# Reordering queues around embedding tiles, the last MLP pair and the gate weights of a two-layer decoder trunk

## The chip, the cores and the metric

One core of one Trainium2 chip. The metric is the device time of one execution in microseconds; the time of a kernel is the median of its runs. TensorE (PE) multiplies, with a queue of weight loads (PEld) beside it; VectorE (DVE), ScalarE (ACT) and GpSimd (POOL) work on tiles; SyncE (SP) issues most DMA loads and stores.

## The reference, cut to what matters

Two layers on 512 tokens of 1024 features, everything in float32. Each layer has a mixer, an MLP and a gated embedding:

```python
for i in range(DEPTH):
    hn = rmsnorm(h, norm_mix_g[i])
    h = h + (even_mixer(hn, ...) if i % 2 == 0 else odd_mixer(hn, ...))
    hn = rmsnorm(h, norm_mlp_g[i])
    u = jnp.square(jax.nn.relu(hn @ w_mlp_up[i]))
    h = h + u @ w_mlp_down[i]
    gate = jax.nn.sigmoid(rmsnorm(h, norm_ple_g[i]) @ w_ple_gate[i])
    h = h + (p[i] @ w_ple_proj[i]) * gate
return rmsnorm(h, final_norm_g)
```

The even mixer has eight stick-breaking heads (groups 0 and 1 of four heads) and four differential heads (groups 2 and 3); the odd mixer has sixteen dilated attention heads.

## The kernel before

The residual stream `h` is kept transposed, as eight tiles of 128 features x 512 tokens. To keep float32 accuracy each factor of a matmul is split into a high part (a copy that rounds, on ACT) and a low part (the difference, on VectorE, or on GpSimd in the mixer), and each product is three matmuls, `mm3` (L138, L141, L142): high by high, low by high or high by low, and the other one. `wsplit` (L117 to L129) splits a block of weights that `wload` (L112) has brought in: the copy is L122, the difference L126 on GpSimd or L128 on VectorE. Raw weights have two buffers, split ones ("wh", "wl") three. `split_tile` (L175 to L184) does the same for a tile of `h`.

**Mixer.** `project` makes the values, queries and keys of one group while `attend` works on the group before; `interleave` mixes the two in program order. For each key tile `evacuate` (L478 to L499) scales the accumulator into one tile "tmp", and for each of its two heads makes two copies `kh` (L495, L496) on ACT and one difference `klz` (L497) on VectorE. In layer 0 `ple_units` (L355 to L373) follows directly behind the keys of groups 0 and 1: it multiplies the embedding by its projection, eight tiles of 128 x 512 one after another in the two "mm" banks; each is copied out by ACT (L372) and stored by SyncE (L373) for the gate stage.

**MLP.** The hidden features are worked in four chunks of four blocks. `up(ch, c)` makes two accumulators, each passed through a relu (L738, VectorE) and a square (L739, ACT), then differences T1 to T4 (L744 to L748, for a multiplication scheme with seven products in place of eight) and their split: `uh` (L750, ACT) and `ul` (L751, VectorE). `down(ch, c)` multiplies a chunk by its four w_down blocks; it sums and splits weights (L789 on ACT, L790 on VectorE), and the last one for a column block takes the last hidden block in a pass of its own, so that TensorE can begin before `uh` and `ul` are there. `side_sums` (L888) and `finished` add what was collected beside and split the finished tiles of `h` (L182, L183) for the next norm, whose squares are L241 and whose sums are L247 (a DMA add), L250, L251 and L254. `down_last` (L856 to L874) makes the last two tiles of `h` with plain products (L871).

**Gate.** Layer 0 (`ple_t`) takes the gate weights in four blocks and the accumulators as tiles of features; `Norm.finish` (L256 to L264) and `rsqrt` (L209 to L216: logarithm L210, exponential L213, then three VectorE steps L214, L215, L216) give the norm's root. Layer 1 (`ple_final`) turns to rows of tokens: for each half of the columns four split blocks, contracted in the order block, then token tile, in the first half, and token tile, then block, in the second; `turn` transposes `h` (L943, copied by L944), `tok_cols` (L281 to L287) transposes the root (L284) to a column per token tile, and the evacuation is sigmoid (L994), product (L995), sum (L996) and square (L997).

**What sets the order.** Each engine works through its queue in order. The queues are laid out ahead of time by the scheduler of the framework, which follows the program's order but lets a later instruction go first where, by its own reckoning, the earlier one isn't ready. `order(later, earlier)` (L224) pins two instructions of one engine against each other without a semaphore.

Of the kernel before, what the change touches and what calls it, by code (L numbers as in the profile page):

```python
# [62 lines left out]
def trunk(  # L63
# [53 lines left out]
    def wsplit(raw, i, nk, n, pool=None):  # L117
# [4 lines left out]
        nc.scalar.activation(hi, src, AF.Copy)  # L122
# [4 lines left out]
        else:  # L127
            nc.vector.tensor_tensor(lo, src, hi.bitcast(F32), op=ALU.subtract)  # L128
        return hi, lo  # L129

# [78 lines left out]
    def rsqrt(y, t, mean, eps, eps_t, scale=1.0, tables=None):  # L209
# [3 lines left out]
        nc.scalar.activation(y, y, AF.Exp, scale=-0.5)  # L213
        nc.vector.tensor_tensor(t, y, y, op=ALU.mult)  # L214
        nc.vector.scalar_tensor_tensor(t, mean, eps / scale, t, op0=ALU.add, op1=ALU.mult)  # L215
        nc.vector.scalar_tensor_tensor(y, t, 3.0 / scale, y, op0=ALU.subtract, op1=ALU.mult)  # L216
# [7 lines left out]
    def order(later, earlier):  # L224
        tc.add_manual_dep(
            later, earlier.name,
            mybir.DependencyInfo(mybir.DependencyClass.NoSync, mybir.DependencyReason.DATA),
            reason="activation tables")

    class Norm:  # L230
# [8 lines left out]
        def stats(self, k, after=(), dma=None, defer=None):  # L239
# [13 lines left out]
            else:  # L253
                nc.vector.tensor_tensor(self.acc, self.acc, sq, op=ALU.add)  # L254
# [100 lines left out]
    def ple_units(layer):  # L355
# [4 lines left out]
        for c in range(2):  # L360
            wh, wl = wsplit(raw, c, 2, 512)
            for i in range(4):
# [10 lines left out]
                nc.sync.dma_start(pjd[layer, 4 * c + i], t)  # L373

    KLB = 2
# [3 lines left out]
    def mixer(layer, norm, nxt):  # L379
# [35 lines left out]
        def project(g, cur):  # L415
# [62 lines left out]
            def evacuate(isq, i, acc, qk, qscale):  # L478
# [12 lines left out]
                else:  # L491
                    for s, (a, b) in enumerate(((lower, upper), (upper, lower))):
                        kl = klz[s][kl_i[0] % KLB]
                        kh = mpool.tile([P, S], F32R, tag="kh", name=nm("kh"), bufs=5)
                        nc.scalar.activation(kh[a], f[a], AF.Copy)  # L495
                        nc.scalar.activation(kh[b], f[a], AF.Copy)  # L496
                        nc.vector.tensor_tensor(kl[a], f[a], kh[a].bitcast(F32), op=ALU.subtract)  # L497
                        heads.append((qk[i][s], kh, kl))
                    kl_i[0] += 1  # L499
# [211 lines left out]
    def mlp(layer, fpool, norm, nxt):  # L711
# [4 lines left out]
        hidden, spare, stages, b12, low, lows = {}, [], [], [], [], []  # L716

        def up(ch, c):
# [16 lines left out]
            ul = fpool.tile([P, 7, HW], F32R, tag="ul", name=nm("ul"), bufs=5)  # L735
            for i, acc in enumerate(accs):
                ui = u[:, B11 + 2 * i:B11 + 2 * i + 2].rearrange("p a c -> p (a c)")
                nc.vector.scalar_tensor_tensor(ui, acc, 0.0, rstd[0], op0=ALU.max, op1=ALU.mult)  # L738
                nc.scalar.activation(ui, ui, AF.Square, scale=0.5)  # L739
# [8 lines left out]
            nc.vector.scalar_tensor_tensor(  # L748
# [3 lines left out]
            hidden[ch, c] = (uh, ul, part.ins)  # L752
# [9 lines left out]
        def down(ch, c):  # L762
# [19 lines left out]
            def split(src):  # L782
# [6 lines left out]
                nc.scalar.activation(hi, src, AF.Copy)  # L789
# [37 lines left out]
            w24 = split(s24)  # L827
            lows.append(low[0])
# [6 lines left out]
            for ks in ((0, 1, 2), (3,)) if last and c == 0 else (range(4),):  # L835
# [11 lines left out]
                if w is None:  # L847
                    w = split(rv[:, A12:A22 + 1])
                product(2, 0, w, 0, B21, False, True, ks)
# [6 lines left out]
        def down_last(c):  # L856
            blk = block(w_down[layer, 4 * (NCH - 1) + c], KT, P)
            low.clear()
            defer = []
            finished(c - 1)  # L860
            for i, (wh, wl) in enumerate(blk):
                acc = ps_wide()
                for m in range(4):
                    uh, ul = hidden[NCH - 1, m][:2]
                    bh, bl = b12[m]
                    for r, rows in enumerate((((acc[:, 0:HW], uh[:, B11], ul[:, B11]), (acc[:, HW:S], bh, bl)),
                                              ((acc, *(x[:, B21:B22 + 1].rearrange("p a c -> p (a c)") for x in (uh, ul))),))):
                        k = 2 * m + r
                        for lh, x in ((wh, 1), (wh, 2), (wl, 1)):
                            for row in rows:  # L870
                                nc.tensor.matmul(row[0], lh[:, k], row[x], start=k == 0 and x == 1 and lh is wh and row is rows[0],  # L871
                                                 stop=k == KT - 1 and lh is wl)
# [245 lines left out]
```

## Time and profile before

| | |
|---|---|
| median of 3 runs | 1305.18 us (1303.14 to 1307.39) |
| the profiled execution's own time | 1305.36 us |
| its span, first to last instruction | 1303.6 us |
| TensorE busy | 1277.1 us |
| VectorE, ACT, GpSimd busy | 1005.1, 710.2, 213.2 us |
| mean granted TensorE clock | 0.996 |

The span is the time from the first to the last instruction that the profiler saw. A timeline row gives the start, the duration, the engine, the line in the kernel, the operation, what it writes and reads, the shapes, and in brackets how long the engine had stood idle and whom it waited for. A row of the waits gives the total, the times and the longest.

### The profile page before, as it was taken

The numbers are of one execution on the slowest core, as the hardware profiler recorded it, in microseconds if no ns is written. First come the engines' busy times: TensorE is split into PE (matmuls) and PEld (weight loads), VectorE is DVE, ScalarE is ACT, GpSimd is POOL, SyncE is SP. The second block draws the span as 40 slices with busy tenths as digits, with TensorE's granted clock in tenths as the row PEclk, the third lists the DMA queues.
The fourth block names the chain that finished last, engine by engine and source line by source line (L and its number), as shares of the span: only waits on it lengthen the run. The fifth ranks groups of instructions, "written<-read, shape, count | busy, mean of one in ns | idle before, by whom it ended". The sixth has DMA issues, their size and how long they took to land.

```text
span 1303.6 us, 19326 instructions
## 1 busy us (share of the span) xinstructions
PE 1277.1 (98%) x7520; PEld 1125.7 (86%) x7520; DVE 1005.1 (77%) x1673; ACT 710.2 (54%) x1149; POOL 213.2 (16%) x184
## 2 busy tenths in 40 slices
PE   9999999999999999999999999999999999999996
PEld 7988887888988989988889888788899898998975
DVE  6788798778858869679767777887785885976876
ACT  6666867555535344355456666764553433534644
POOL 2433533400000000001023333231000000000201
PEclk9999999999999999999999999999999999999998
DMA  6421423222232322646432222212323133254741
GB/s 213 140 81 61 151 74 113 89 98 97 98 99 96 117 103 77 189 116 172 173 130 82 81 89 82 65 58 97 101 94 129 65 103 124 85 163 141 170 145 65
DMA packets 33996, 144.25 MB, mean 111 GB/s; under 512 B 3889, under 2 KB 4625, under 8 KB 21233
## 3 DMA queue, kind: packets, MB, share of 16 engines
q1 hardware_dynamic: 29680, 135.16, 30.6%
q0 software_dynamic: 4224, 7.87, 3.5%
q8 instruction: 59, 0.97, 0.3%
q14 instruction: 33, 0.26, 0.1%
HBM read 131.92 MB, written 6.37 MB: 106 GB/s over the span
## 4 chain that ended last, share of the span: by engine, by line
PE 76%; DVE 11%; ACT 5%; DMA 4%; issue 3%; POOL 0%; SPq 0%; ACTq 0%; DVEq 0%; POOLq 0%
PE mm L138 11%; PE mm L142 10%; PE mm L141 10%; PE sc L141 5%; PE sc L142 5%; PE sc L138 5%; PE pv L142 4%; PE pv L141 4%; PE pv L138 4%; PE tp L142 4%; PE tp L141 4%; PE tp L138 4%; PE pv L558 3%; PE tp L539 2%; DMA side<-u 2%
## 5 line engine op out<-in xcount | busy, mean ns | idle before, releaser
L122 ACT ACTIVATE wh<-raw 128x1024 fp32r<-128x1024 f32 (+1 forms) x156 | 160.5, 1034 | 142.7 <-PE mm L141 47.9
L126 POOL TENSOR_TENSOR wl<-raw,wh 128x512 fp32r<-128x512 f32 (+1 forms) x132 | 178.3, 1373 | 304.1 <-ACT wh L122 304.1
L138 PE MATMUL mm<-hi,wh 128*128 128x512 f32 x472 | 187.1, 396 | 0.2 <-ACT pjt L372 0.2
L142 PE MATMUL mm<-hi,wl 128*128 128x512 f32 x472 | 185.0, 392 | 1.6 <-DVE wl L128 1.5
L141 PE MATMUL mm<-lo,wh 128*128 128x512 f32 x472 | 184.6, 391 | 0.0
L128 DVE TENSOR_TENSOR wl<-raw,wh 128x1024 fp32r<-128x1024 f32 x90 | 109.4, 1221 | 46.4 <-ACT wh L122 40.8
L142 PEld LDWEIGHTS mm<-hi,wl 128*128 128x128 f32 x472 | 88.6, 188 | 22.2 <-DVE wl L128 2.2
L138 PEld LDWEIGHTS mm<-hi,wh 128*128 128x128 f32 x472 | 88.7, 188 | 16.8 <-ACT pjt L372 0.4
L141 PEld LDWEIGHTS mm<-lo,wh 128*128 128x128 f32 x472 | 88.8, 188 | 15.6
L760 POOL DMA_DIRECT2D s<-in_w_down_dram x4 | 4.5, 1123 | 579.1 <-DMA s<-in_w_down_dram 313.2
L789 ACT ACTIVATE wh<-s 128x1024 fp32r<-128x1024 f32 x58 | 61.1, 1053 | 52.8 <-DVE s L776 14.7
L751 DVE TENSOR_TENSOR ul<-u,uh 128x1792 fp32r<-128x1792 f32 x32 | 64.8, 2024 | 31.9 <-ACT uh L750 31.8
L533 ACT ACTIVATE e<-e,mn 128x128 f32<-128x128 f32 (+3 forms) x96 | 53.8, 561 | 62.3 <-DVE mn L530 61.9
L790 DVE TENSOR_TENSOR wl<-s,wh 128x1024 fp32r<-128x1024 f32 x58 | 70.8, 1221 | 13.9 <-ACT wh L789 13.5
L750 ACT ACTIVATE uh<-u 128x1792 fp32r<-128x1792 f32 x32 | 54.5, 1703 | 48.4 <-DVE u L748 48.2
L739 ACT ACTIVATE u<-u 128x512 f32<-128x512 f32 x64 | 39.7, 626 | 68.0 <-DVE u L738 67.8
L141 PE MATMUL sc<-lo,wh 128*128 128x512 f32 x184 | 72.1, 392 | 0.3 <-DVE lo L183 0.3
L138 PE MATMUL sc<-hi,wh 128*128 128x512 f32 x184 | 72.2, 392 | 0.1
L142 PE MATMUL sc<-hi,wl 128*128 128x512 f32 x184 | 71.9, 391 | 0.0
L138 PE MATMUL mm<-wh,hi 128*128 128x256 f32 (+1 forms) x216 | 63.2, 292 | 0.0
L142 PE MATMUL mm<-wh,lo 128*128 128x256 f32 (+1 forms) x216 | 62.9, 291 | 0.0
L141 PE MATMUL mm<-wl,hi 128*128 128x256 f32 (+1 forms) x216 | 62.8, 291 | 0.0
(305 smaller groups left out, 3887.1 us busy)
## 6 DMA issues: line engine op xcount, KB each, us to landing
raw<-in_w_up_dram SPq DMA_DIRECT2D x32, 1024.0 KB, 4.9
raw<-in_w_down_dram SPq DMA_DIRECT2D x32, 1024.0 KB, 4.9
raw<-in_w_in_dram SPq DMA_DIRECT2D x23, 1024.0 KB, 4.9
raw<-in_w_gate_dram SPq DMA_DIRECT2D x8, 1024.0 KB, 6.0
bias<-urow SPq DMA_DIRECT2D x24, 256.0 KB, 3.6
raw<-in_w_outa_dram SPq DMA_DIRECT2D x8, 768.0 KB, 4.2
pj<-pjd SPq DMA_DIRECT2D x16, 256.0 KB, 5.7
h<-in_xT_dram SPq DMA_DIRECT2D x8, 256.0 KB, 5.7
```

Of the source, the lines that this page charges most:

```text
L122: nc.scalar.activation(hi, src, AF.Copy)
L126: nc.gpsimd.tensor_tensor(lo[:, kx], src[:, kx], hi[:, kx].bitcast(F32), op=ALU.subtract)
L128: nc.vector.tensor_tensor(lo, src, hi.bitcast(F32), op=ALU.subtract)
L138: mm = nc.tensor.matmul(acc, lh, rh, start=start, stop=False)
L141: nc.tensor.matmul(acc, lh, rl, start=False, stop=False)
L142: return mm.ins, nc.tensor.matmul(acc, ll, rh, start=False, stop=stop).ins
L533: nc.scalar.activation(e[:, 0:n], e[:, 0:n], AF.Exp, scale=-1.0, bias=mn, accum_out=s)
L739: nc.scalar.activation(ui, ui, AF.Square, scale=0.5)
L750: nc.scalar.activation(uh, u, AF.Copy)
L751: part = nc.vector.tensor_tensor(ul, u, uh.bitcast(F32), op=ALU.subtract)
L789: nc.scalar.activation(hi, src, AF.Copy)
L790: low[:] = [nc.vector.tensor_tensor(lo, src, hi.bitcast(F32), op=ALU.subtract).ins]
```

## The change

It has three parts. First, in layer 0 the copies of the last key tile's second head of groups 0 and 1 (and the difference behind them) are no longer emitted with the first head's, but by `ple_units` just behind the first embedding tile's copy and store. Second, in the MLP the low half of the second weight pair of `down(3, 0)` is ordered behind the first relu of `up(3, 3)`, the high half of its third pair behind the second square and the low half of that behind T4. Third, `down_last` loads and splits the first gate block itself, between its two accumulators; `finished(2)` comes behind that, its side sums ordered behind the first gate low half, the squares' sums behind the second. In layer 1 the last gate block's splits are ordered behind the root (high halves behind the exponential, low halves behind the last step), two of the split blocks swap pools, and `tok_cols` is emitted behind two token tiles of the fourth block instead of ahead of it.

```diff
@@ ple_units, mixer @@
                 nc.sync.dma_start(pjd[layer, 4 * c + i], t)
+                while late_copies:
+                    late_copies.pop()()
...
-                        nc.scalar.activation(kh[a], f[a], AF.Copy)
-                        nc.scalar.activation(kh[b], f[a], AF.Copy)
-                        nc.vector.tensor_tensor(kl[a], f[a], kh[a].bitcast(F32), op=ALU.subtract)
+
+                        def copies(a=a, b=b, kh=kh, kl=kl):
+                            nc.scalar.activation(kh[a], f[a], AF.Copy)
+                            nc.scalar.activation(kh[b], f[a], AF.Copy)
+                            nc.vector.tensor_tensor(kl[a], f[a], kh[a].bitcast(F32), op=ALU.subtract)
+
                         heads.append((qk[i][s], kh, kl))
+                        if i and s and layer == 0 and g in groups[2:]:
+                            late_copies.append(copies)
+                        else:
+                            copies()
@@ Norm.stats @@
-                nc.vector.tensor_tensor(self.acc, self.acc, sq, op=ALU.add)
+                add = nc.vector.tensor_tensor(self.acc, self.acc, sq, op=ALU.add)
+                for a in late_add:
+                    order(add.ins, a)
@@ up, down @@
-                nc.vector.scalar_tensor_tensor(ui, acc, 0.0, rstd[0], op0=ALU.max, op1=ALU.mult)
-                nc.scalar.activation(ui, ui, AF.Square, scale=0.5)
+                chain.append(nc.vector.scalar_tensor_tensor(ui, acc, 0.0, rstd[0], op0=ALU.max, op1=ALU.mult).ins)
+                chain.append(nc.scalar.activation(ui, ui, AF.Square, scale=0.5).ins)
...
-            hidden[ch, c] = (uh, ul, part.ins)
+            hidden[ch, c] = (uh, ul, part.ins, chain[0], chain[3], t4.ins)
...
             w24 = split(s24)
+            if last and c == 0:
+                order(low[0], hidden[ch, 3][3])
...
                     w = split(rv[:, A12:A22 + 1])
+                    if last and c == 0:
+                        order(high[0], hidden[ch, 3][4])
+                        order(low[0], hidden[ch, 3][5])
@@ down_last @@
-            low.clear()
             defer = []
-            finished(c - 1)
...
+                if i == 0:
+                    raw = wload(w_gate[layer, 0])
+                    n = (KT, P) if layer < DEPTH - 1 else (2, 512)
+                    gate.append(wsplit(raw, 0, *n))
+                    low[:] = last_low
+                    gate.append(wsplit(raw, 1, *n))
+                    late_add[:] = last_low
+                    finished(c - 1)
                 nc.vector.tensor_tensor(h[2 * c + i], h[2 * c + i], acc, op=ALU.add)
                 nxt.done(2 * c + i, defer=defer)
+            late_add.clear()
@@ ple_t @@
-            blk = block(w_gate[layer, c], KT, P)
+            blk = gate if c == 0 else block(w_gate[layer, c], KT, P)
@@ ple_final @@
-            gw = []
-            for half in range(2):
+            gw = [] if c else list(gate)
+            for half in range(1 - c, 2):
                 raw = wload(w_gate[layer, 2 * c + half])
                 for b in range(2):
-                    gw.append(wsplit(raw, b, 2, 512, pool=fpool if c else None))
+                    gw.append(wsplit(raw, b, 2, 512, pool=None if (c, half, b) in ((0, 1, 0), (1, 1, 1)) else fpool))
+                    if c and half:
+                        order(last_high[0], root[0])
+                        order(last_low[0], root[1])
...
                     for t in range(QT):
                         contract(t, b, 0)
+                        if b == 3 and t == 1:
+                            rcol = tok_cols(rstd)
...
                     if b == 2:
-                        rcol = tok_cols(norm.finish())
+                        rstd = norm.finish()
                         turn(1)
```

`last_low`, `last_high` and `root` hold the instructions of the latest `wsplit` and `rsqrt`.

21 lines of the change are left out of this document (14 added, 7 removed).

## The prediction

> **What bounds the kernel now.** I read the page first, then the waits of TensorE, then the timeline of each engine around each wait that the edits touch.
>
> ```profile
> PE 1277.1 (98%) x7520; PEld 1125.7 (86%) x7520; DVE 1005.1 (77%) x1673; ACT 710.2 (54%) x1149; POOL 213.2 (16%) x184
> ```
>
> TensorE is busy for 98% of the span, so the change, which removes no arithmetic, can only return time in which TensorE stands still. The waits of TensorE say how much that is and who ends it (total us, times, longest):
>
> ```profile
> PE mm L138 <- ACT tmp L372: 2.6, 2, 1.4
> PE mm L141 <- DVE ul L751: 2.0, 2, 1.0
> PE tp L284 <- DVE rstd L216: 1.7, 1, 1.7
> ...
> PE mm L142 <- DVE wl L128: 1.5, 1, 1.5
> ...
> PE mm L142 <- DVE wl L790: 0.8, 2, 0.4
> ```
>
> Each of the first four belongs to one part of the diff, so I take them as parts A, B, E and D. The fifth (C, in the third w_down pair) isn't edited, but comes just behind B.
>
> **A: the last key tile's second head.** The two waits are at the start of the two embedding runs, in layer 0. The first:
>
> ```profile
> 140.59 0.63 ACT L495 ACTIVATE kh<-tmp 64x512 fp32r<-64x512 f32 x1
> 141.24 0.63 ACT L496 ACTIVATE kh<-tmp 64x512 fp32r<-64x512 f32 x1
> 141.78 0.57 ACT L372 ACTIVATE tmp<-mm 128x512 f32<-128x512 f32 x1
> ...
> 141.00 0.22 PE L516 MATMUL sc<-masks 128*128 128x128 f32 x1
> 142.40 0.50 PE L138 MATMUL mm<-wh,wh 128*128 128x512 f32 x1 [1.18 <-ACT tmp L372]
> 142.74 0.39 PE L141 MATMUL mm<-wl,wh 128*128 128x512 f32 x1
> 142.97 0.40 PE L142 MATMUL mm<-wh,wl 128*128 128x512 f32 x1
> ```
>
> The third embedding tile needs one of two "mm" banks; the copy that frees it (L372) stands on ACT behind the two copies of the second head (140.59 and 141.24). With those two deferred, L372 starts at 140.59 and ends at 141.16. The second site has the same order:
>
> ```profile
> 203.28 0.63 ACT L495 ACTIVATE kh<-tmp 64x512 fp32r<-64x512 f32 x1
> ...
> 204.46 0.57 ACT L372 ACTIVATE tmp<-mm 128x512 f32<-128x512 f32 x1
> ...
> 203.36 0.33 PE L513 MATMUL sc<-kh,qq 128*128 128x256 f32 x1
> 205.09 0.50 PE L138 MATMUL mm<-wh,wh 128*128 128x512 f32 x1 [1.40 <-ACT tmp L372]
> ```
>
> There L372 would end at 203.28 + 0.57 = 203.85 instead of 205.03.
>
> What a wait costs is more than its bracket. Rows of L138 to L142 with 512 columns last 0.39 and start 0.23 apart (142.74 to 142.97), so 0.16 of a matmul normally lies under the next one; and the first one behind the wait is followed after 0.34 (142.40 to 142.74), 0.11 more than normal. So each wait costs its bracket plus 0.27, by starts alone. The Trainium skill ("Perfetto Trace Analysis", section on the Tensor Engine Instruction) says that the end of a matmul row is estimated from its size and not observed; the trace agrees, as the rows overlap. By the brackets alone A, B, D and E would sum to 7.75, by starts to 9.26.
>
> A by starts: 1.18 + 1.40 + 2 × 0.27 = 3.12. What is late next: TensorE is free at about 141.05 and 203.55, so 0.1 and 0.3 of a wait stay. And the deferred pair (2 × 0.65 by its spacing) now stands ahead of the second embedding tile's copy: 141.16 + 1.30 + 0.57 = 143.0, where the fourth tile asks for its bank at 141.2 + 6 × 0.23 = 142.6. That is up to 0.4 per site. I take 0.55 returned per site, A = 2.0; ends 0.8 and 3.1. The deferred VectorE subtraction goes with the copies; the scores of that head are twelve steps away, and SyncE's store of the first embedding tile only moves earlier.
>
> **B: orders around the last pair.** Layer 1, last up block and the first w_down block behind it:
>
> ```profile
> 1195.39 1.22 DVE L790 TENSOR_TENSOR wl<-s,wh 128x1024 fp32r<-128x1024 f32 x1
> 1196.53 0.69 DVE L738 SCALAR_TENSOR_TENSOR u<-pv,rstd 128x512 f32<-128x512 f32 x1
> ...
> 1199.37 1.23 DVE L790 TENSOR_TENSOR wl<-raw,wh 128x1024 fp32r<-128x1024 f32 x1
> 1200.51 0.69 DVE L744 TENSOR_TENSOR u<-u 128x512 f32<-128x512 f32 x1
> ...
> 1202.21 1.70 ACT L750 ACTIVATE uh<-u 128x1792 fp32r<-128x1792 f32 x1 [2.10 <-DVE u L748]
> ...
> 1203.94 2.02 DVE L751 TENSOR_TENSOR ul<-u,uh 128x1792 fp32r<-128x1792 f32 x1 [1.83 <-ACT uh L750]
> ...
> 1197.15 0.28 PE L138 MATMUL mm<-uh,wh 128*128 128x256 f32 x1
> ...
> 1204.70 0.28 PE L138 MATMUL mm<-uh,wh 128*128 128x256 f32 x1
> 1206.03 0.39 PE L141 MATMUL mm<-ul,wh 128*128 128x256 f32 x1 [1.04 <-DVE ul L751]
> ```
>
> The chain to ul is relu (L738), square, differences, L750, L751. Two low halves of weights (1195.39 and 1199.37, 1.2 each) stand in it. The orders put the first behind the first relu, the second behind the last difference, where VectorE waits 1.83 for L750 anyway. The first relu starts at 1195.39; the second one's accumulator is complete just behind 1197.15, where the w_down block begins, so with some 0.5 for what VectorE still does there it ends near 1198.4. Its square is as long as the relu (0.7), the differences take 1202.21 - 1200.51 = 1.70 up to L750: near 1200.8. L750 1.70 and L751 2.02 end near 1204.6, before 1204.98 where ul is wanted. Who waits for the moved halves: the first now ends near 1196.53 + 0.69 + 0.1 = 1197.3, and its product comes third in the w_down block, behind two of nine matmuls each; the 63 matmuls from 1197.15 to 1204.70 start 0.12 apart, so at 1199.3. The second ends near 1200.8 + 1.23 = 1202.0; its product is the sixth, at 1197.15 + 45 × 0.12 = 1202.6. The raw buffer that it releases comes free 1.4 later, and with it the next SyncE load, whose block begins only after all of this one. Behind the halves on VectorE and ACT stand only members of the same chain. B by starts: 1.97 + 2 × 0.27 = 2.51; I take 2.4, ends 0 (the chain moves by nothing) and 2.5.
>
> C starts from TensorE's own results (copies out of the banks, a DMA add, side sums), so it should move along. If it is bound by loads instead, it grows by what B saves. I charge 0.5 for both layers; ends +1.3 (0.8 + 2 × 0.27 gone) and -2.4 (all of B given back).
>
> **D: early gate weights.**
>
> ```profile
> 610.04 1.04 ACT L122 ACTIVATE wh<-raw 128x1024 fp32r<-128x1024 f32 x1
> ...
> 614.58 1.22 DVE L128 TENSOR_TENSOR wl<-raw,wh 128x1024 fp32r<-128x1024 f32 x1
> ...
> 607.43 0.28 PE L871 MATMUL tp<-uh,wh 128*128 128x256 f32 x1
> ...
> 613.07 0.39 PE L138 MATMUL mm<-hi,wh 128*128 128x512 f32 x1
> ...
> 615.85 0.50 PE L142 MATMUL mm<-hi,wl 128*128 128x512 f32 x1 [1.46 <-DVE wl L128]
> ```
>
> In layer 0 the second gate block's low half is made at 614.58, though its high half ended at 611.08: h updates and splits are ahead of it on VectorE. Emitted in the middle of the last w_down block and with the squares' adds ordered behind it, it needs only its load, which keeps its place, and the weight buffer that the first half of that block frees at 607.43, where the second begins. So it ends near 607.6 + 1.04 + 1.22 = 609.9, ahead of the gate product at 613.07, and 1.46 + 0.27 = 1.73 goes. What is now behind the first gate low half, the side sums of tiles 4 and 5 and with them their splits, is wanted by the fifth of eight steps of the gate product, 4 × 6 × 0.23 = 5.5 behind 613.07; behind the second stand only sums for the norm, which is read after the whole product. Tiles 4 and 5 use no DMA add, so POOL isn't concerned. In layer 1 there is no such wait and I count 0. D = 1.7, ends 1.0 and 1.8.
>
> **E: the last gate block behind the root.**
>
> ```profile
> 1259.80 2.01 ACT L122 ACTIVATE wh<-raw 128x1024 fp32r<-128x1024 f32 x2 [8.68 <-DMA raw<-in_w_gate_dram]
> 1261.71 0.67 ACT L210 ACTIVATE rstd<-tp,eps_n 128x512 f32<-128x512 f32 x1
> ...
> 1264.61 0.69 DVE L216 SCALAR_TENSOR_TENSOR rstd<-e,rstd 128x512 f32<-128x512 f32 x1
> ...
> 1259.64 0.40 PE L262 MATMUL tp<-e,ones_r 128*128 128x512 f32 x1
> ...
> 1265.45 0.63 PE L284 MATMUL tp<-ident,rstd 128*128 128x128 f32 x4 [1.74 <-DVE rstd L216]
> ```
>
> ```profile
> L944 DVE COPY ht<-tp 128x512 f32<-128x512 f32 x8 | 5.3, 687 | 0.6 <-PE tp L943 0.6
> ```
>
> The two high halves run ahead of the logarithm, whose input is complete at 1259.64 + 0.40 and a little, say 1260.1. Ordered behind the root they give 1261.71 - 1260.1 = 1.6: rstd is ready near 1263.7 instead of 1265.3, and moving tok_cols behind two token tiles of the fourth contraction lets transposes of h go first. E by starts: 1.74 + 0.16 = 1.90 (no refill there, as the transposes are short); I take 1.4, because h copies of 0.69 (L944) may now slip between the root's three steps; ends 0.5 and 1.9. The new places of two split blocks (one out of the shared weight buffers, one into them) I count at nothing: the block that leaves them no longer waits for a buffer, so the load behind it, which landed at 1259.8, comes earlier, and its split is now held by the root in any case.
>
> **Sum.** 2.0 + 2.4 - 0.5 + 1.7 + 1.4 = 7.0. The profiled execution took 1305.36, 0.18 above the median 1305.18 of the runs; its waits stand for all. So 1298.4 for such an execution, 1298.2 as the median, 0.54% less. A measurement of this kernel can tell about 0.3% (3.9 us) from no change.
>
> **The rivals.** One: waits change hands. The deferred pair blocks the fourth embedding tile, and the pair's low halves or C give B back. For it: ACT's rows at both sites of A follow each other without a gap, and C lies one block behind B. Against: the room reckoned above. D and E stay: 1305.18 - 3.1 = 1302.1.
>
> Two, slower: the low halves of the last gate block, now behind the root, fall behind the evacuation of the first 512 columns, whose adds come earlier in the program.
>
> ```profile
> 1269.63 0.40 PE L138 MATMUL tp<-wh,hi 128*128 128x512 f32 x1
> ...
> 1279.53 0.69 DVE L996 TENSOR_TENSOR ht<-ht,gt 128x512 f32<-128x512 f32 x1
> ```
>
> The last column tiles begin at 1269.63 and want the halves after twelve matmuls, at 1272.4. Made behind the last add they are ready at 1280.2 + 2 × 1.22 = 1282.6: a wait of 10.2, so 1298.2 + 10.2 = 1308.4, with A and C at their poor ends up to 1311.5. It decides once the halves end after 1272.4, that is, from the second evacuated token tile on. Against it: the halves can be made as soon as the root is there, before rcol exists and so before any sigmoid. The Trainium skill ("TensorE: Matmul & The Clock Gate", architectural detail) says that ScalarE and VectorE take their queues strictly in order; the trace agrees at 141.78, and by that rule nothing can overtake a half that is placed late.
>
> Three: the deferral and the orders leave the queues as they are, and only D acts: 1305.18 - 1.7 = 1303.5.
>
> **How the numbers follow.** Forecast 0.72 (0.70 of it over 0.3% faster), rival one 0.16 (0.02 faster, 0.14 within), rival two 0.07 (0.05 slower, 0.02 within), rival three 0.05 (within). Faster 0.72, same 0.23, slower 0.05. The low end is all 9.26 returned and nothing given back, 1295.9. The high end takes in rival one with its 0.5 of spread, 1302.6; rivals two and three are outside.
>
> **What would show it.** In the waits of TensorE, L372, L751, L216 and L128 gone or under 0.5 each; L372 ahead of the second head's L495; L738 ahead of the first L790; L128 for the second gate block ending before 611; L210 ahead of the last two L122. A new wait on L372 or a larger one on L790 would mean rival one; a wait of TensorE on L128 behind 1265 would mean rival two. A TensorE busy time that differs from 1277.1 by more than 2 would make the whole reckoning wrong.

## The result, and the profile after

| | before | after |
|---|---|---|
| median | 1305.07 us (6 runs, 1303.14 to 1307.39) | 1296.33 us (6 runs, 1295.27 to 1298.25) |
| ratio to before | | 0.9932, 95% interval 0.992 to 0.9945 |
| the profiled execution, its span | 1305.36, 1303.6 | 1296.47, 1294.7 |
| end of the last matmul, stretch from there to the end of the span | 1291.87, 11.68 | 1285.31, 9.39 |

The change is faster by 8.7 us, 0.68%. The forecast was 1298.2 in a range of 1295.9 to 1302.6. The sum of 7.0 fell short by 1.7, and not because every term was a little small. Between the two profiled executions the last matmul ends 6.56 us earlier, 0.44 less than the sum. The other 2.29 us lie behind the last matmul, in a place that the prediction did not look at.

The page of the changed kernel first, then its waits of TensorE (total us, times, longest):

```profile
PE 1277.1 (99%) x7520; PEld 1125.5 (87%) x7520; DVE 1003.3 (77%) x1673; ACT 710.0 (55%) x1149; POOL 212.5 (16%) x184
```

```profile
PE mm L141 <- ACT tmp L381: 1.1, 2, 0.8
...
PE mm L145 <- DVE wl L810: 0.7, 2, 0.4
...
PE mm L144 <- DVE ul L771: 0.2, 1, 0.2
```

(The lines have moved: the three matmuls of `mm3`, L138, L141 and L142, are now L141, L144 and L145, L247 is now L254, L372 is L381, L495 and L496 are L509 and L510, L738 is L758, L790 is L810, L750 and L751 are L770 and L771, L210 to L216 are L213 to L219, L284 is L293, L943 and L944 are L976 and L977, L950 is L983, L994 to L997 are L1032 to L1035, L254 is L261, the "fin" steps of L272 are L281.) TensorE is as busy as before, so the reckoning in idle time holds. The wait on the root (L216) and the one on the gate's low half (L128) are gone, L751's 2.0 is 0.2, C's 0.8 is 0.7. Of A's 2.6 there is still 1.1. Take the same matmul in both traces by its number in TensorE's order: the lead is how much earlier it starts after the change. It grows to 1.25 by 280 us (A), from 1.27 to 2.08 at 578 (B, layer 0), from 1.99 to 3.74 at 616 (D), from 3.57 to 4.42 at 1206 (B, layer 1), from 4.54 to 4.86 at 1253 (a wait on a copy of h that is gone), and from there to 6.56 at the last matmul (E). Between these places it drifts by 0.1 to 0.2.

The timeline of the changed kernel at the four places:

```profile
140.52 0.60 ACT L381 ACTIVATE tmp<-mm 128x512 f32<-128x512 f32 x1
...
141.14 0.63 ACT L509 ACTIVATE kh<-tmp 64x512 fp32r<-64x512 f32 x1
...
141.17 0.50 PE L141 MATMUL mm<-wh,wh 128*128 128x512 f32 x1 [0.37 <-ACT tmp L381]
...
142.96 0.19 PEld L141 LDWEIGHTS mm<-wh,wh 128*128 128x128 f32 x1 [0.33 <-ACT pjt L381]
142.96 0.50 PE L141 MATMUL mm<-wh,wh 128*128 128x512 f32 x1
...
202.24 0.61 ACT L510 ACTIVATE kh<-tmp 64x512 fp32r<-64x512 f32 x1
...
202.88 0.60 ACT L381 ACTIVATE tmp<-mm 128x512 f32<-128x512 f32 x1
...
203.53 0.50 PE L141 MATMUL mm<-wh,wh 128*128 128x512 f32 x1 [0.77 <-ACT tmp L381]
...
608.43 1.22 DVE L128 TENSOR_TENSOR wl<-raw,wh 128x1024 fp32r<-128x1024 f32 x1
...
1192.46 0.69 DVE L758 SCALAR_TENSOR_TENSOR u<-pv,rstd 128x512 f32<-128x512 f32 x1
1193.07 1.21 DVE L810 TENSOR_TENSOR wl<-s,wh 128x1024 fp32r<-128x1024 f32 x1
...
1197.62 1.22 DVE L810 TENSOR_TENSOR wl<-raw,wh 128x1024 fp32r<-128x1024 f32 x1
1197.79 1.70 ACT L770 ACTIVATE uh<-u 128x1792 fp32r<-128x1792 f32 x1 [0.78 <-DVE u L768]
...
1201.61 0.39 PE L144 MATMUL mm<-ul,wh 128*128 128x256 f32 x1 [0.20 <-DVE ul L771]
...
1255.20 0.69 ACT L213 ACTIVATE rstd<-tp,eps_n 128x512 f32<-128x512 f32 x1 [10.16 <-PE tp L271]
...
1256.46 1.99 ACT L122 ACTIVATE wh<-raw 128x1024 fp32r<-128x1024 f32 x2
1256.59 0.69 DVE L217 TENSOR_TENSOR e<-rstd 128x512 f32<-128x512 f32 x1 [0.26 <-ACT rstd L216]
1257.20 0.68 DVE L977 COPY ht<-tp 128x512 f32<-128x512 f32 x1
...
1259.24 0.68 DVE L219 SCALAR_TENSOR_TENSOR rstd<-e,rstd 128x512 f32<-128x512 f32 x1
...
1260.07 0.63 PE L293 MATMUL tp<-ident,rstd 128*128 128x128 f32 x4
```

Each order that the prediction asked to see is there: the embedding copy ahead of the second head's copies, the first relu ahead of the low half, the gate's low half done before 611, the logarithm ahead of the last two high halves. One of its signs isn't met: of the waits that were to go or fall under 0.5, the second one on L381 is 0.77. Three places are to be kept in mind: at the first site of A the fourth embedding tile (142.96) has waited for its bank (the 0.33 of its weight load), at the second site the first head's second copy (202.24) stands ahead of L381, and a copy of h (1257.20) has slipped between the root's steps.

Where the unforeseen 2.29 come from is seen in the last evacuation. Before, ScalarE and the last matmul:

```profile
1283.57 0.73 ACT L950 ACTIVATE ht<-ht,fin 128x512 f32<-128x512 f32 x1 [2.60 <-DVE fin L272]
1284.20 0.67 ACT L994 ACTIVATE gt<-tp,rcol 128x512 f32<-128x512 f32 x1
...
1289.68 0.72 ACT L950 ACTIVATE ht<-ht,fin 128x512 f32<-128x512 f32 x1 [2.60 <-DVE fin L272]
1290.31 0.67 ACT L994 ACTIVATE gt<-pv,rcol 128x512 f32<-128x512 f32 x1
...
1291.60 0.28 PE L142 MATMUL mm<-wh,lo 128*128 128x256 f32 x1
...
1295.02 0.45 ACT L994 ACTIVATE gt<-mm,rcol 128x256 f32<-128x256 f32 x1
```

After:

```profile
1274.68 0.67 ACT L1032 ACTIVATE gt<-tp,rcol 128x512 f32<-128x512 f32 x1
...
1278.39 0.73 ACT L983 ACTIVATE ht<-ht,fin 128x512 f32<-128x512 f32 x1 [0.18 <-DVE fin L281]
...
1279.66 0.69 ACT L1032 ACTIVATE gt<-pv,rcol 128x512 f32<-128x512 f32 x1 [0.54 <-PE pv L145]
...
1285.04 0.28 PE L145 MATMUL mm<-wh,lo 128*128 128x256 f32 x1
...
1286.16 0.46 ACT L1032 ACTIVATE gt<-mm,rcol 128x256 f32<-128x256 f32 x1
```

Before, each scaled copy (L950) waits 2.60 for a chain of small VectorE steps ("fin") and the next tile's sigmoid stands behind it; the sigmoids come 1290.31 - 1284.20 = 6.1 apart. The last one starts 3.4 behind the start of the last matmul. The Trainium skill ("TensorE: Matmul & The Clock Gate", architectural detail) says that ScalarE takes its queue strictly in order; the trace agrees, since a sigmoid starts right behind each scaled copy (1284.20 behind 1283.57, 1290.31 behind 1289.68). After, the second tile's sigmoid (1274.68) stands ahead of the first tile's scaled copy (1278.39), the third's waits for TensorE itself (0.54 on pv), and the last one starts 1.1 behind the start of the last matmul. No line of the diff names these instructions.

### The profile page after: what moved, and what is told of

Its sections match the earlier page's. It is cut to its first block, busy times and chain, and to the rows that moved or that the text cites. A ratio compares the mean times of both kernels' runs of the same rounds, so it can differ in the third digit from the quotient of the medians.

```text
span 1294.7 us, 19322 instructions
## 1 busy us (share of the span) xinstructions
PE 1277.1 (99%) x7520; PEld 1125.5 (87%) x7520; DVE 1003.3 (77%) x1673; ACT 710.0 (55%) x1149; POOL 212.5 (16%) x184
## 4 chain that ended last, share of the span: by engine, by line
PE 80%; DVE 10%; ACT 4%; DMA 2%; issue 2%; POOL 0%; SPq 0%; ACTq 0%; DVEq 0%; POOLq 0%
PE mm L141 11%; PE mm L144 11%; PE mm L145 11%; PE sc L144 5%; PE sc L145 5%; PE sc L141 5%; PE pv L145 4%; PE pv L144 4%; PE pv L141 4%; PE tp L145 4%; PE tp L144 4%; PE tp L141 4%; PE pv L577 3%; PE tp L558 2%; PE tp L894 2%
## 5 line engine op out<-in xcount | busy, mean ns | idle before, releaser
L141 PE MATMUL mm<-hi,wh 128*128 128x512 f32 x472 | 187.1, 396 | 0.2 <-ACT pjt L381 0.2
L145 PE MATMUL mm<-hi,wl 128*128 128x512 f32 x472 | 184.8, 391 | 0.1
L144 PE MATMUL mm<-lo,wh 128*128 128x512 f32 x472 | 184.6, 391 | 0.0
L128 DVE TENSOR_TENSOR wl<-raw,wh 128x1024 fp32r<-128x1024 f32 x90 | 109.6, 1222 | 39.6 <-ACT wh L122 34.1
L145 PEld LDWEIGHTS mm<-hi,wl 128*128 128x128 f32 x472 | 88.6, 188 | 20.0 <-POOL wl L126 0.5
L141 PEld LDWEIGHTS mm<-hi,wh 128*128 128x128 f32 x472 | 88.7, 188 | 16.9 <-ACT pjt L381 0.4
L144 PEld LDWEIGHTS mm<-lo,wh 128*128 128x128 f32 x472 | 88.8, 188 | 15.5
L771 DVE TENSOR_TENSOR ul<-u,uh 128x1792 fp32r<-128x1792 f32 x32 | 64.8, 2024 | 29.6 <-ACT uh L770 29.5
L810 DVE TENSOR_TENSOR wl<-s,wh 128x1024 fp32r<-128x1024 f32 x58 | 70.8, 1221 | 12.6 <-ACT wh L809 12.2
L770 ACT ACTIVATE uh<-u 128x1792 fp32r<-128x1792 f32 x32 | 54.5, 1703 | 45.7 <-DVE u L768 45.4
L144 PE MATMUL sc<-lo,wh 128*128 128x512 f32 x184 | 72.3, 393 | 0.4 <-DVE lo L186 0.4
L141 PE MATMUL sc<-hi,wh 128*128 128x512 f32 x184 | 72.2, 392 | 0.0
L145 PE MATMUL sc<-hi,wl 128*128 128x512 f32 x184 | 71.9, 391 | 0.0
L141 PE MATMUL mm<-wh,hi 128*128 128x256 f32 (+1 forms) x216 | 63.4, 293 | 0.0
L145 PE MATMUL mm<-wh,lo 128*128 128x256 f32 (+1 forms) x216 | 63.0, 292 | 0.0
L144 PE MATMUL mm<-wl,hi 128*128 128x256 f32 (+1 forms) x216 | 62.9, 291 | 0.0
```

The lines of the kernel that those rows point to most:

```text
L128: last_low[:] = [nc.vector.tensor_tensor(lo, src, hi.bitcast(F32), op=ALU.subtract).ins]
L141: mm = nc.tensor.matmul(acc, lh, rh, start=start, stop=False)
L144: nc.tensor.matmul(acc, lh, rl, start=False, stop=False)
L145: return mm.ins, nc.tensor.matmul(acc, ll, rh, start=False, stop=stop).ins
L770: nc.scalar.activation(uh, u, AF.Copy)
L771: part = nc.vector.tensor_tensor(ul, u, uh.bitcast(F32), op=ALU.subtract)
```

## The experiments

Two questions were open: what each part is worth by itself, and what shortened the stretch behind the last matmul. Theory T said ScalarE's queue order there; the rival R said the earlier root and evacuation. Times of a set stand beside runs of the kernel before in the same set: 1306.89 (17 runs) for the first four, 1306.79 (11) for the next four, 1306.53 (13) for the last four. The changed kernel, run again in the last set, is the yardstick for times (medians of different sets are compared, and those of the kernel before differ by up to 0.36); the stretch behind the last matmul is read from each profiled execution.

**The changed kernel again.**

> The changed kernel itself, as the yardstick for the others of this set: 1296.3 within 1.5, the stretch behind the last matmul 9.4. In some executions the third DMA add of squares of the last norm may land late (its sum in VectorE waited 7.3 and 7.4 us instead of 2 in two executions of other kernels), which would show as a wait of 3 to 4 at the transposes of h and a time near 1301.

Measured: 1297.19 (5 runs), ratio 0.9924 (0.9912 to 0.9936), stretch 9.39.

**The tail forced back (T against R).**

```diff
+            scaled.append(cp)
...
                     sg = nc.scalar.activation(gt, ..., AF.Sigmoid, ...)
+                    if scaled:
+                        order(sg.ins, scaled[-1].ins)
```

> The changed kernel with one thing put back: in the last column half the sigmoid of each next token tile is ordered behind the scaled copy (L983) of the tile before, as ScalarE's queue had it before the change. TensorE's queue is untouched. Theory T (the stretch behind the last matmul shrank by 2.3 us because ScalarE takes the second tile's sigmoid ahead of the first tile's scaled copy): last matmul where it is in the changed kernel (1285.3 within 0.3), the stretch from it to the end of the span back from 9.4 to 11.7, so 1296.3 + 2.3 = 1298.6. Rival R (the stretch shrank because the root and the whole evacuation come earlier): the order changes nothing, 1296.3 within 0.5, stretch 9.4.

Measured: stretch 11.16, time 1298.5, ratio 0.994 (0.9928 to 0.9952). Of the 2.29 the order gives back 1.77, with TensorE's queue untouched and the earlier root in place; in its trace the scaled copies wait 2.60 again and the sigmoids come 6.1 apart (1279.65, 1285.76). So R, by which nothing would change, falls; where the other 0.52 comes from stays open. The last matmul ends at 1286.94 and not at 1285.3 as expected, 1.0 of it for a drop of the clock that the last section describes, so here the stretch tells more than the time.

**The tail's ScalarE order alone, in the kernel before.**

```diff
                     sg = nc.scalar.activation(gt, ..., AF.Sigmoid, ...)
+                    if c and not i and 0 < t < QT - 1:
+                        finish(*done.pop(), (sg,))
...
-                if t < QT - 2:
-                    finish(*done.pop())
```

> The kernel before with one thing added: the scaled copy of the first and of the second token tile stands on ScalarE behind the next tile's sigmoid, as in the changed kernel; nothing of A, B, D or E. Theory T: the stretch behind the last matmul (1291.9 within 0.3) shrinks from 11.7 to 9.4, so 1305.1 - 2.3 = 1302.8. Rival R: the stretch stays at 11.7 and the time at 1305.1 within 0.5.

Measured: stretch 10.23, 1.45 less, where T wanted 2.3; time 1305.99, ratio 0.9997 (0.9987 to 1.0007), which can't be told from no change. In its trace the first tile's whole fin chain and scaling still stand ahead of the second tile's product on VectorE, and the sigmoids come 5.4 apart (1282.97, 1288.35, 1293.73), where the changed kernel's VectorE makes the second tile's product (1276.03) between two steps of that chain. So ScalarE's order alone is worth 1.45 of the 2.29. That the time didn't follow has a reason in the trace: the last matmul ends at 1293.95 instead of 1291.87, for here TensorE stood 2.5 for a copy of h at 1257 (0.2 in the kernel before), and the clock dropped once.

**Both queues cut, in the kernel before (T2).**

```diff
-        for _ in range(3):
-            newton(dst, x, t)
+        newton(dst, x, t)
+        def rest(after):
+            for _ in range(2):
+                order(newton(dst, x, t), after)
+        return rest
...
                     ad = nc.vector.tensor_tensor(hs, hs, gt, op=ALU.add)
+                    if rests and i == len(parts[t]) - 1:
+                        rests.pop()(ad.ins)
+                        if not last:
+                            finish(*done.pop(), (sg,))
```

> The kernel before with the loop of the last evacuation cut on both engines: of each token tile's final root only the first of three Newton steps stays ahead of the next tile's product and sum on VectorE, the other two are ordered behind that sum, and the scaled copy on ScalarE stands behind the next tile's sigmoid. Nothing of A, B, D or E. Theory T2 (the loop sigmoid, product, sum, square, thirteen small steps, scaled copy, next sigmoid took 6.1 per tile where TensorE takes 5.5; with both queues cut the evacuation keeps up with TensorE): the stretch behind the last matmul is 8.2 to 9.4 instead of 11.7, 1305.1 to 1306.9 for the kernel before becomes 2.3 to 3.5 less. If ScalarE's order alone matters (theory T): 10.2, as in the run with that order alone, 1.5 less.

Measured: stretch 8.75, time 1303.09 (9 runs), ratio 0.9977 (0.9966 to 0.9987). Its ScalarE rows and last matmul (the sigmoid is L1001 here):

```profile
1288.95 0.69 ACT L1001 ACTIVATE gt<-pv,rcol 128x512 f32<-128x512 f32 x1 [0.38 <-PE pv L142]
...
1294.32 0.28 PE L142 MATMUL mm<-wh,lo 128*128 128x256 f32 x1
...
1294.70 0.47 ACT L1001 ACTIVATE gt<-mm,rcol 128x256 f32<-128x256 f32 x1 [0.39 <-PE mm L142]
```

Now these sigmoids wait for TensorE (0.38, 0.39) and no longer for the tile before. With nothing of A to E the stretch shrinks by 2.9, inside the range that T2 gave. T2 holds: the loop through both engines made the tail.

**No orders behind the root.**

```diff
-                    if c and half:
-                        order(last_high[0], root[0])
-                        order(last_low[0], root[1])
```

> The changed kernel without the orders that hold the last gate block's splits behind the root; the transposes of the root still come behind two token tiles of the fourth block. Theory E1 (the later place of the transposes, with sixteen transposes of h ahead of them, carries the gain of part E, since three copies of h slipped into the root's chain and left the orders only about 0.5): a wait of 0.4 to 0.9 at the transposes of the root, 1296.3 + 0.6 = 1296.9. Rival E2 (the orders carry it, as forecast): a wait of 1.7 and about 1298.0. By T the stretch behind the last matmul stays at 9.4, since the second tile's sigmoid still stands ahead of the scaled copy.

Measured: 1297.41 (6 runs, 1296.71 to 1302.55), ratio 0.994 (0.9924 to 0.9957), 0.2 above the yardstick; stretch 9.24. Its profiled execution has no wait at the root's transposes, but it can't tell E1 from E2, since another wait, 8 us ahead of the sum matmuls, gave the halves time to be made before the root was asked for:

```profile
PE tp L976 <- DVE ht L977: 4.0, 1, 4.0
```

```profile
1241.59 0.69 DVE L261 TENSOR_TENSOR rstd<-rstd,e 128x512 f32<-128x512 f32 x1 [7.44 <-DMA rstd<-side]
```

By the time E1 is nearer (1296.9 expected, against 1298.0), but the runs scatter by more than the two differ; how much the orders add to the cover stays open.

**The root's transposes at their old place.**

```diff
-                        if b == 3 and t == 1:
-                            rcol = tok_cols(rstd)
...
-                        rstd = norm.finish()
+                        rcol = tok_cols(norm.finish())
```

> The changed kernel with the transposes of the root at their old place, ahead of the transposes of h; the orders behind the root stay. With no copy of h ahead in VectorE's queue the root should end about 4.0 behind the start of the last sum matmul, where 3.7 of matmuls cover it. E1: either piece alone is nearly enough, a wait of 0.2 to 0.6 at these transposes. E2 says the same here; no cover at all would be a wait over 1.5. The scheduler puts the first scaled copy ahead of the second tile's sigmoid again in this kernel, so by T the stretch behind the last matmul is 11.7 and the time 1296.3 + 0.4 + 2.3 = 1299.0; by R it is 9.4 and 1296.7.

```profile
1257.50 0.69 DVE L219 SCALAR_TENSOR_TENSOR rstd<-e,rstd 128x512 f32<-128x512 f32 x1
...
1258.34 0.63 PE L293 MATMUL tp<-ident,rstd 128*128 128x128 f32 x4
...
1277.07 0.72 ACT L983 ACTIVATE ht<-ht,fin 128x512 f32<-128x512 f32 x1 [2.60 <-DVE fin L281]
1277.70 0.67 ACT L1030 ACTIVATE gt<-tp,rcol 128x512 f32<-128x512 f32 x1
```

Measured: time 1298.83, ratio 0.9942 (0.993 to 0.9953); no wait of TensorE at L293, so the orders behind the root are enough without the cover: from the start of the last sum matmul (1254.23) to the end of the root it takes 4.0, where the kernel before took 5.7. The last matmul ends at 1284.81. But the scaled copy is ahead of the sigmoid again, waits 2.60 again, and the stretch is 12.24. So in the changed kernel the moved `tok_cols` line is what makes the scheduler lay out the tail in the other order (whether it does so by itself, without the other parts, no run shows): none of the other kernels made from the changed one by leaving a part out lost it (stretches of 9.24 to 9.79).

**Part A undone.**

```diff
-                        if i and s and layer == 0 and g in groups[2:]:
+                        if False:
```

> The changed kernel without part A: both heads' copies of the last key tile are emitted together again. Theory T1 (the parts add up, A returned 1.25 because the first head's second copy still stands ahead of the first embedding tile's copy): the two waits on L381 go from 1.1 back to 2.6, time 1296.3 + 1.2 = 1297.5. Rival (the deferral itself is worth the 2.0 that was forecast and something else took 0.8 of it): +2.0, 1298.3, with the waits at 2.6 and a smaller wait elsewhere.

Measured: the waits on L381 are 2.6 again, time 1297.87, ratio 0.9936 (0.9924 to 0.9948), 0.7 above the yardstick. That is nearer to the 1.25 of the trace than to 2.0, but the intervals of the two ratios overlap. By the traces, the lag behind the changed kernel's first profile grows from 0.48 at 139 us to 1.72 at 400, by 1.24.

**Part A carried further.**

```diff
-                while late_copies:
-                    late_copies.pop()()
+                if late_copies:
+                    late_copies.pop(0)(cp)
...
+                                if cp is not None:
+                                    order(k.ins, cp.ins)
...
-                        if i and s and layer == 0 and g in groups[2:]:
+                        if i and layer == 0 and g in groups[2:]:
```

> The changed kernel with part A carried further: the first head's copies of the last key tile are ordered behind the first embedding tile's copy too, the second head's behind the second embedding tile's copy. T1: the copy that frees the bank starts 0.65 earlier at both sites, both waits on L381 at the third tile go under 0.2, time 1296.3 - 1.1 - 0.3 = 1294.9. Rival (the copies block the next embedding tile's copy, the new wait that the prediction feared): a wait of 0.4 to 0.8 on the second embedding tile's copy per site, time 1295.5 to 1296.5.

```profile
PE mm L141 <- ACT tmp L381: 1.3, 1, 1.3
...
PE sc L534 <- ACT e L619: 0.9, 1, 0.9
```

Measured: 1298.31, ratio 0.9944 (0.9929 to 0.9958), 1.1 above the yardstick. At the first site the wait of 0.37 is gone, and 0.89 is waited 4 us later for an exponential that the copies pushed back. At the second site the scheduler put another copy (of an attention output) ahead of L381, so the wait there grew to 1.30. The waits change hands, though not at the tile that I had named. (Its profiled execution was the slowest of the six, 1303.13; the last section says why.)

**Part B undone.**

```diff
-            if last and c == 0:
-                order(low[0], hidden[ch, 3][3])
...
-                    if last and c == 0:
-                        order(high[0], hidden[ch, 3][4])
-                        order(low[0], hidden[ch, 3][5])
```

> The changed kernel without part B: the three orders around the last pair of low halves are gone. T1: the two waits on L771 go from 0.2 back to 2.0, the waits on L810 stay at 0.7, time 1296.3 + 1.8 = 1298.1. Rival (the third pair is bound by something that doesn't move along, so B was partly given back there): the waits on L810 shrink to under 0.3 and the time rises by 1.2 or less.

```profile
PE mm L144 <- DVE ul L771: 2.6, 2, 1.5
...
PE mm L145 <- DVE wl L810: 0.8, 2, 0.4
```

Measured: 1299.08, ratio 0.9948 (0.9936 to 0.996), 1.9 above the yardstick; by the traces 0.9 at 578 us and 1.3 at 1203. C's wait stays at 0.8 with or without B: it moves along with TensorE and gives nothing back.

**Part D undone.**

```diff
+            low.clear()
+            finished(c - 1)
             for i, (wh, wl) in enumerate(blk):
...
-                if i == 0:
-                    raw = wload(w_gate[layer, 0])
...
-            blk = gate if c == 0 else block(w_gate[layer, c], KT, P)
+            blk = block(w_gate[layer, c], KT, P)
...
-            gw = [] if c else list(gate)
+            gw = [] if c else block(w_gate[layer, 0], 2, 512)
```

> The changed kernel without part D: the first gate block is loaded and split in the gate stage again, and the collected sums come ahead of the last w_down block; the order behind the root stays. T1: the wait on L128 at the first gate block of layer 0 comes back with 1.5, time 1296.3 + 1.5 = 1297.8; in layer 1 nothing changes. Rival (the early block also feeds part E, since the last gate block's load waits for a buffer that the early one frees): 1.5 and up to 1.4 more, with a wait behind 1250 that the changed kernel doesn't have.

```profile
610.19 0.69 DVE L261 TENSOR_TENSOR rstd<-rstd,e 128x512 f32<-128x512 f32 x1 [2.59 <-DMA rstd<-side]
...
613.32 1.22 DVE L128 TENSOR_TENSOR wl<-raw,wh 128x1024 fp32r<-128x1024 f32 x1
...
1246.91 1.06 ACT L122 ACTIVATE wh<-raw 128x1024 fp32r<-128x1024 f32 x1 [3.01 <-DMA raw<-in_w_gate_dram]
...
1249.75 1.22 DVE L128 TENSOR_TENSOR wl<-raw,wh 128x1024 fp32r<-128x1024 f32 x1
1250.89 1.28 DVE L971 COPY ht<-tp 128x512 f32<-128x512 f32 x2
```

Measured: 1301.18, ratio 0.9963 (0.995 to 0.9976), 4.0 above the yardstick, far more than 1.5; between its profile and the changed kernel's first one it is 3.05 up to the last matmul and 0.40 behind it. Its waits of TensorE say where: 2.5 on the gate's low half in layer 0, 1.0 on a copy of h at 1252, and a stretch of 9.79. The first is the wait that D removes, longer than in the kernel before, because a sum of squares ahead of the low half on VectorE stood 2.59 for a DMA add (0.72 in the profile of before). The second is the rival's: without the early block the next gate load comes late (3.01 of ScalarE's waiting), its low halves come late, and the copies of h stand behind them.

**The third DMA add made by VectorE.**

```diff
-                nc.gpsimd.dma_start(self.acc, sq, accum_op=ALU.add)
+                if k == 3:
+                    self.held = sq
+                else:
+                    nc.gpsimd.dma_start(self.acc, sq, accum_op=ALU.add)
```

> The changed kernel with the third of the three DMA adds of squares (the fourth feature tile's) made by VectorE, right ahead of the next sum there, in both layers; the same values are summed. Theory L (the executions that are 4 to 5 us longer come from that third DMA add landing late, with VectorE's queue standing behind it): no execution over 1299, the sum waits under 2.5, no wait over 0.5 at the transposes of h; the median within 0.7 of the changed kernel's. Rival (the long executions come from elsewhere): some run over 1300 again, or the median rises by the 0.7 that the added step takes on VectorE.

Measured: 1297.68 (1296.31 to 1298.27, 5 runs), ratio 0.9927 (0.9914 to 0.9941). No execution over 1299, but the changed kernel had none either in its eleven, so theory L is neither shown nor refuted by it. In its trace the sum that takes the add's place (1236.06) waits for nothing. The median moved by 0.5, less than the runs scatter.

**Both edits on the changed kernel.**

> The changed kernel with the last two edits together: the third DMA add made by VectorE, and the split of the final roots. By T2 and L: the stretch behind the last matmul 8.2 to 9.0 instead of 9.4, so 1296.3 - 0.4 to 1.2 = 1295.1 to 1295.9, and no execution over 1299. If VectorE is simply full in this stretch (its steps behind the second tile's sum are 7.9 us long), the stretch stays at 9.4 or grows by up to 0.5.

(The diffs are those of the two edits shown.) Measured: 1296.16 (1295.38 to 1296.62, 4 runs), ratio 0.9918 (0.9904 to 0.9931), stretch 8.76 where the changed kernel has 9.39. The 0.63 is in the trace; the intervals of the two ratios overlap, so the times don't show it to be faster than the changed kernel.

## Why the prediction was right, and where it wasn't

**The direction and the mechanism** were right: TensorE was 98% busy, the change gave back idle time alone, and idle time went at each of the four places that were priced, at two of them wholly (D, E). Busy time stayed at 1277.1. That the sum came out within 0.44 up to the last matmul is partly luck: A and B fell short by 0.75 each, and the 0.5 charged for C, the 0.3 that E gave above its price and the 0.4 of D made up for most of it.

**A, 2.0 forecast, 1.25 in the trace, 0.7 by undoing it.** The deferral did what was said. The step that failed is "TensorE is free at about 141.05 and 203.55, so 0.1 and 0.3 of a wait stay": 0.37 and 0.77 stayed. It took the end of TensorE's work from the order of before, and the scheduler now puts only three score matmuls instead of six ahead of the third tile at the first site, and none instead of four at the second. There, moreover, ScalarE's copies start only 0.41 earlier than before (201.09 against 201.50) while TensorE arrives at 202.76 instead of 203.69; so the first head's second copy, which wasn't deferred, is now the one that is late. The feared wait of the fourth tile did come, at the first site: its matmul has no bracket, but its weight load waited 0.33 for the copy, and it starts 0.29 behind the matmul ahead of it, where such a one is otherwise followed after 0.12. At the two sites the lead grows by 0.35 and 0.60; the other 0.2 came at 279.5, where the kernel before and the one without A lose it at a matmul without a bracket.

**B, 2.4 forecast, 1.66 in the trace, 1.9 by undoing it.** The low halves left the chain as meant, but 0.20 of the wait on ul stayed in layer 1 and 0.12 in layer 0. The step that failed is "with some 0.5 for what VectorE still does there": the second relu starts at 1194.70, 1.12 behind the start of the w_down block (1193.58), since the moved low half (1193.07, 1.21) and a difference of 0.42 are still ahead of it. What stays varies: the waits on L771 sum to 0.9 in the yardstick's profile, and to between 2.0 and 3.2 in the four profiles without B.

**C, 0.5 charged, nothing given back.** Its wait is 0.7 after, 0.8 with B undone.

**D, 1.7 forecast, 1.75 in layer 0, and 0.32 more** at 1253 by the lead. I counted layer 1 at nothing, since no wait stood there on the gate weights; the early load moved the later ones, which the d_undo run shows by their absence. By undoing it D is worth 4.0, since its wait grows when a DMA add lands late. The step "h updates and splits are ahead of it on VectorE" left out the sum that waits for that add.

**E, 1.4 forecast, 1.70 in the trace.** Copies of h did slip between the root's steps, as feared: from the start of the last sum matmul (1254.78) to the end of the root takes 5.1 where it took 5.7 before: the orders gave 0.5 of the 1.6 that was reckoned for them, and the h transposes that now come ahead covered the rest. Where no copy slips in (the run with `tok_cols` at its old place) it takes 4.0, and the orders give the whole 1.7.

**The start-up of a wait, 0.27 each, came back only where the wait went as a whole.** At D it did: the lead grows by 1.75 for a bracket of 1.46, as "each wait costs its bracket plus 0.27, by starts alone" has it. At B a small wait is left in both layers, the first row behind it is as long as before (0.39), and the lead grows by 0.81 and 0.85, the differences of the brackets alone. At A a wait is left at both sites, too, and the fourth tile's start-up is new. So what was wrong is counting 2 × 0.27 in full for A and for B. The room that I had left below the starts hid this.

**The rivals.** No wait on the last gate block's low halves came behind 1265 (two), and more than D acted (three). Waits did change hands in part (one), but only in A (the fourth tile).

**The tail, nothing forecast, 2.29.** The step that failed is the sum itself: it let everything behind the root move along rigidly. The 2.60 waits of L950 were in the profile of before, but the prediction looked only at waits of TensorE and stopped at its last matmul. Without the 2.29 the median would have been 1298.6, next to the 1298.2 that was forecast. The change of order is the scheduler's answer to one moved line (the run with `tok_cols` at its old place), and the gain is that of cutting a loop of 6.1 per tile (the runs with the tail forced back and with both queues cut).

## What to carry to other kernels

Behind the last matmul look for a loop through two in-order queues, such as sigmoid, product, square, root, scaled copy and the next sigmoid, and compare its period with TensorE's per tile: here 6.1 against 5.5 (24 matmuls 0.23 apart), and 2.9 us lay in it. Where a scheduler lays out the queues, moving one line can reorder queues that the diff doesn't name, so compare the order of every queue from there to the end. And price a removed wait with what is late next in the new order of both engines; carrying both over from the old trace made A 2.0 where 1.25 came. A wait that only shrinks keeps its start-up.

## What the runs showed of the hardware

How long a DMA add takes differs between executions. In the last norm GpSimd issues three adds of squares one behind the other; from the issue of the second to VectorE's sum behind the third it took 11.5 us in the changed kernel's profile, and 17.3 in the one without orders behind the root (10.1 in the kernel before, 16.6 with part A carried further):

```profile
1224.42 0.86 POOL L254 DMA_DIRECT2D rstd<-side  x1 [1.54 <-ACT side L248]
1232.40 0.86 POOL L254 DMA_DIRECT2D rstd<-side  x1 [7.13 <-ACT wh L122]
...
1235.89 0.69 DVE L261 TENSOR_TENSOR rstd<-rstd,e 128x512 f32<-128x512 f32 x1 [2.09 <-DMA rstd<-side]
```

```profile
1224.28 0.86 POOL L254 DMA_DIRECT2D rstd<-side  x1 [1.54 <-ACT side L248]
1234.18 0.86 POOL L254 DMA_DIRECT2D rstd<-side  x1 [9.05 <-DVE wl L128]
```

From the third one's issue to that sum it is 3.5 and 7.4 (the sum without the orders is the row at 1241.59 above). There it left TensorE standing for 4.0 (the wait on L977 above), and the execution took 1302.55 where the same kernel's median is 1297.41. What delays the add was not found.

The granted clock can drop for a moment, too. Two windows (busy us of each engine, granted clock, DMA share, GB/s), of the yardstick's profile and of the one without orders behind the root:

```profile
838.60:841.90 3.30, 3.30 (x12) 2.91 (x11) 2.57 (x5) 2.19 (x5) 2.18 (x2) 0.50 0.00 0
```

```profile
1250.60:1257.40 6.80, 4.92 (x16) 4.16 (x17) 4.96 (x8) 2.15 (x3) 0.00 (x0) 0.50 0.50 190
```

At 0.50 matmuls of 512 columns start 0.43 apart (840.52, 840.95, 841.37 in the first, 1255.53, 1255.96, 1256.38 in the second) instead of 0.23. In the first, TensorE had just stood 1.3 and 0.5 at an attention product; three other profiles show the same drop of 3.4 us there, and ten with the same two waits do not. Because of it the stretch from the 4000th to the 5000th matmul took 173.6 us instead of 172.7, nearly as much as part A is worth.

In the second, the clock fell during the standstill of 4.0, for 6.8 us. The lag behind the changed kernel grew by 4.1 at the wait and by 2.3 more at the lower clock, so the wait cost 6.4, over half as much again as its bracket. The profile with part A carried further has the same behind a standstill of 3.2. Behind the one of 2.5 in the run without part D the clock stayed at 1.00. Parts of this size are read from the trace by place and not from two times.
